# Five transposed parameter vectors leave VectorE for ScalarE, and attention's score products take the two key groups in turn

## The chip, the cores and the metric

The kernel runs on one core of a Trainium2 chip. The metric is the device time of one execution in microseconds (us); shorter is better. A core has TensorE (matmuls; PE in the profile, with PEld for its weight loads), VectorE (DVE), ScalarE (ACT), GpSimd (POOL) and SyncE (SP), which here only issues DMAs. Each engine works through its own list of instructions in order, and engines wait for each other by semaphores. Matmul results land in PSUM, in banks of 512 floats per partition.

## The reference, cut to what matters

Two layers of a decoder trunk are computed on 512 tokens of width 1024. Layer 0 has a mixer (windowed attention beside a gated short convolution), a gated MLP with a width-3 convolution, and an embedding gate. Layer 1 has the same with gated linear attention as its mixer. The attention of layer 0 is where the change acts:

```python
qb = q.reshape(b, nb, ATTN_BLOCK, ATTN_KV_HEADS, ATTN_GROUP, HEAD_DIM)   # 4 blocks of 128 queries, 2 key groups, 4 heads each, 64 wide
scores = jnp.einsum('bnqhgd,bnkhd->bnhgqk', qb, kband).astype(jnp.float32) * (HEAD_DIM ** -0.5)
...
scores = jnp.where(allowed[None, :, None, None], scores, -jnp.inf)
...
probs = jax.nn.softmax(jnp.concatenate([scores, sink], axis=-1), axis=-1)[..., :-1]
```

Each block of 128 queries sees its own 128 keys and the 128 before them (the first block only its own). The change also touches how small parameter vectors (norm gains, convolution taps and biases) come to stand along the partitions.

## The kernel before, in words

Activations stand transposed, features on partitions and the 512 tokens along the free axis. The large projections are done by `mm3` (lines 149 to 155) in three products on split operands, high by high (L153) and the two crosses of a high and a low part (L154, L155). The weights come by DMA as `raw` and are split by `cut`: ScalarE makes the high part `wh` (L133), VectorE the rest `wl` (L134). Such products, 512 wide, are the bulk of TensorE's work, and they go to PSUM tiles named `ps` (four banks). Everything smaller, transposes and attention, goes to tiles named `pa`, which are also four banks, handed round: a new `pa` tile must wait until the reader of the tile that held its bank before has finished.

`columns` (L182 to L195) turns parameter vectors: DMAs gather rows into `vrow`, TensorE transposes them into a `pa` tile (L192), and VectorE copies the result out of PSUM (L194). It is called six times: once at the start for `vec0` (with a queue given as `q`), once in mixer 0 for `vec1`, and twice in each `load_vectors_ffn` for `vfa` and `vfb` (in mixer 0 and again in mixer 1).

`mixer0` (from L357) writes its order out by hand at the end (L609 to L650). The convolution's projections (`conv_in`, 48 products each) are laid between the steps of attention so that TensorE has work while the softmax runs on the other engines. The steps are, for each block t of 128 queries:

- `query_turned(t)`: four transposes (L428), then ScalarE copies them to `qT` (L429).
- `scores(t)`: eight products (L492), one per head. Each has 64 rows of contraction: heads of key group 0 lie on partitions 0 to 63, those of group 1 on 64 to 127. Two heads share a `pa` tile, so the step takes four tiles in the order group 0 first pair, group 0 second pair, group 1 first pair, group 1 second pair. In the records each product is two matmuls. VectorE then adds the mask and takes the row maxima, one instruction per head (L500), and prepares the exponent's bias (L507, L508).
- Still in `scores(t)`: ScalarE takes eight exponentials (L514), and VectorE sums and inverts (L518, L519).
- `probs(t)`: the weights are normalized by VectorE (L528) and ScalarE (L532), transposed (L538) and copied to `pT` by ScalarE (L545) and, for the earlier keys, VectorE (L543).
- `mix(t)`: the product with the values (L554), split by ScalarE (L97) and VectorE (L98).

Around `scores(0)` the code says `query_turned(0, qn0)`, `load_vectors1()`, then two more steps, `query_turned(1, qn1)`, `scores(0)`, `conv_in("c", w)`. The `pa` banks of the four score tiles are therefore those that, in turn, the spread norm, `qT` of block 0, the turned `vec1` and `qT` of block 1 held. Within this hand order a scheduler moves single instructions of an engine against each other, so the built order can differ by a few places from the code's. Between the two projections the convolution's own work runs: `conv_taps` multiplies, pads and applies the taps (L588, L589 and L593 on VectorE, L591 on ScalarE), reading `vec1`.

In mixer 1, `load_vectors_ffn(1)` stands right before `read(2)` (L1104): products of scores and values (L1115) and of the state (L1117) into two `pa` tiles, whose squares ScalarE sums (L1119) ahead of the per-head norm; VectorE scales (L1124). A tile's second half may be written only after the squares of its first half were taken. Nearby, ScalarE applies the swish to the output gate (L890) and splits gated outputs (L97), VectorE multiplies (L889, L897).

Of the kernel before, what the change touches and what calls it, by code (L numbers as in the profile page):

```python
# [55 lines left out]
class Kernel:  # L56
# [125 lines left out]
    def columns(self, name, views, q=None):  # L182

        nc = self.nc
        n = sum(v.shape[0] for v in views)
        rows = self.sp.tile([P, P], F32, tag="vrow", name=self.nm("vrow"))
        at = 0
        for v in views:
            (q or nc.gpsimd).dma_start(rows[at : at + v.shape[0], :], v)
            at += v.shape[0]  # L190
        ps = self.pa()
        nc.tensor.transpose(ps[:, :n], rows[:n, :], self.ident[:n, :n])  # L192
        col = self.cp.tile([P, -(-n // 64) * 64], F32, name=name)[:, :n]
        nc.vector.tensor_copy(col, ps[:, :n])  # L194
        return col  # L195

    def load_vectors0(self):
# [159 lines left out]
    def mixer0(self):  # L357
        nc, a, tc = self.nc, self.a, self.tc
        with tc.tile_pool(name="m0", bufs=1) as mp:
# [15 lines left out]
            for m in range(ND):  # L375
                ps = self.ps()
# [103 lines left out]
            def scores(t):  # L480

                w = 2 * P if t else P
                k0 = (t - 1) * P if t else 0
                mask = self.amask if t else self.amask[:, P:]
                s = mp.tile([P, NQ, 2 * P], F32, tag="s", name=self.nm("s"), bufs=2)
                mx = self.few(8, "mx")
                for g in range(2):
                    for h2 in range(2):
                        pb = self.pa()
                        for hh in range(2):  # L490
                            hq = 2 * h2 + hh
                            nc.tensor.matmul(  # L492
                                pb[:, hh * 256 : hh * 256 + w],
                                qTs[t][64 * g : 64 * g + 64, hq, :],
                                kT[64 * g : 64 * g + 64, k0 : k0 + w],
                                start=True, stop=True,
                            )
                        for hh in range(2):
                            head = 4 * g + 2 * h2 + hh
                            nc.vector.tensor_tensor_reduce(  # L500
                                s[:, head, :w], pb[:, hh * 256 : hh * 256 + w], mask,
                                scale=1.0, scalar=-1e30, op0=ALU.add, op1=ALU.max,
                                accum_out=mx[:, head : head + 1],
                            )

                nm = self.few(8, "nm")
                nc.vector.scalar_tensor_tensor(out=nm, in0=mx, scalar=HD**-0.5, in1=sink, op0=ALU.mult, op1=ALU.max)  # L507
                nc.vector.tensor_scalar_mul(nm, nm, -1.0)  # L508
                den = self.few(8, "den")
                es = self.few(8, "es")  # L510
                nc.vector.tensor_tensor(es, sink, nm, ALU.add)
                nc.scalar.activation(es, es, AF.Exp)
                for head in range(NQ):
                    nc.scalar.activation(  # L514
                        s[:, head, :w], s[:, head, :w], AF.Exp, bias=nm[:, head : head + 1], scale=HD**-0.5,
                        accum_out=den[:, head : head + 1],
                    )
                nc.vector.tensor_tensor(den, den, es, ALU.add)  # L518
                nc.vector.reciprocal(den, den)  # L519
                ss[t], dens[t] = s, den  # L520
# [49 lines left out]
            def conv_w(nme, j2):  # L570
                c0 = starts[nme] + 256 * j2
                return self.weights(w_in[:, :, c0 : c0 + 256], ND, 256)
# [36 lines left out]
            w = conv_w("x", 0)  # L609
# [4 lines left out]
            w = conv_w("c", 0)  # L614
# [4 lines left out]
            qn2 = query(2)  # L619
            query_turned(1, qn1)  # L620
            scores(0)
            conv_in("c", w)
            w = conv_w("b", 0)
            conv_taps(0)
            qn3 = query(3)
            query_turned(2, qn2)
            probs(0)
            scores(1)
            conv_in("b", w)
            w = conv_w("x", 1)  # L630
            conv_out(0)
            query_turned(3, qn3)
            mix(0)
            probs(1)
            scores(2)
            conv_in("x", w)
            w = conv_w("c", 1)
# [4 lines left out]
            w = conv_w("b", 1)  # L642
# [639 lines left out]
```

## Time and profile before

| | |
|---|---|
| time, median of 3 runs (lowest to highest) | 1260.3 us (1259.97 to 1260.51) |
| time of the profiled execution | 1260.71 us |
| its span, first to last instruction | 1258.8 us |
| TensorE busy | 99% of the span |
| VectorE busy | 772.7 us, 61% |
| ScalarE busy | 541.1 us, 43% |
| mean granted TensorE clock | 0.999 |
| the five copies of turned vectors in mixers and later (L194) | 0.20 us (vec1), 0.24 us each (vfa, vfb, twice) |
| the 64 records of score products (L492) | 61.3 to 117.0 us of the span |

The span is what the traces divide up; some 1.9 us lie around it (1260.71 less 1258.8). A line of the timeline gives start, length in us, engine, code line, operation, the tiles written and read, their sizes, and in brackets how long the engine had been idle before and what ended that. A matmul's recorded length includes its way through the array, so matmuls that follow each other overlap in the records: a 512-wide product is recorded with 0.39 us, while one starts every 0.23 us. The pace is read from starts.

### The profile page before, as it was taken

The page shows a single profiled execution, that of the slowest core. Times are in us where ns is not written, and L with a number is a line of the kernel's source. Part 1 is how long each engine was busy: PE and PEld are TensorE (multiplying, and loading weights), DVE is VectorE, ACT ScalarE, POOL GpSimd, SP SyncE. Part 2 cuts the span into 40 slices and gives each one's busy share as a digit, 9 for nine tenths or more (in the row PEclk, how much of TensorE's full clock was granted, in tenths as well). Part 3 has the DMA queues.
Part 4 walks back from the last instruction along what each step waited for, and adds up shares of the span by engine and source line. Part 5 has one row for each costly group of instructions (what it writes and reads, how often), then busy time and mean ns, then how long its engine had stood idle before and what let it go on. Part 6 is the DMA issues. An engine that isn't in the chain of part 4 may idle for free.

```text
span 1258.8 us, 14853 instructions
## 1 busy us (share of the span) xinstructions
PE 1244.9 (99%) x5851; PEld 1038.1 (82%) x5851; DVE 772.7 (61%) x1190; ACT 541.1 (43%) x831; POOL 54.1 (4%) x150
## 2 busy tenths in 40 slices
PE   7999999999999999999999999999999999999998
PEld 7777788888888888888989988888888888888887
DVE  6776566777777633346679765557777777433343
ACT  6456344444444422234563544335444444232341
POOL 2500000000000000000100000000000000000000
PEclk9999999999999999999999999999999999999999
DMA  6221232333332233223322222333222233222331
GB/s 212 73 76 55 79 99 93 100 101 101 100 100 92 76 111 99 92 74 101 109 89 67 68 68 67 100 100 102 98 88 86 98 100 101 92 92 93 108 107 61
DMA packets 110473, 117.42 MB, mean 93 GB/s; under 512 B 2712, under 2 KB 105682, under 8 KB 110404
## 3 DMA queue, kind: packets, MB, share of 16 engines
q1 hardware_dynamic: 108512, 114.83, 28.0%
q10 hardware_dynamic: 1332, 1.23, 0.3%
q8 instruction: 46, 0.75, 0.2%
q0 software_dynamic: 560, 0.42, 0.2%
q14 instruction: 23, 0.19, 0.0%
HBM read 114.37 MB, written 2.10 MB: 93 GB/s over the span
## 4 chain that ended last, share of the span: by engine, by line
PE 92%; DVE 3%; ACT 2%; issue 1%; POOL 1%; DMA 1%; SPq 0%; DVEq 0%; POOLq 0%; ACTq 0%
PE ps L153 28%; PE ps L155 28%; PE ps L154 28%; PE pa L492 1%; PE pa L1001 1%; DMA xin<-in_x_dram 1%; PE pa L1115 1%; PE pa L154 1%; DVE wl L134 1%; PE pa L153 1%; PE pa L155 1%; PE pa L538 1%; PE pa L1092 0%; POOL rq L163 0%; PE pa L1117 0%
## 5 line engine op out<-in xcount | busy, mean ns | idle before, releaser
L133 ACT ACTIVATE wh<-raw 128x1024 fp32r<-128x1024 f32 (+4 forms) x222 | 224.7, 1015 | 384.5 <-PE ps L154 319.4
L134 DVE TENSOR_TENSOR wl<-raw,wh 128x1024 fp32r<-128x1024 f32 (+4 forms) x222 | 258.6, 1167 | 184.0 <-ACT wh L133 182.9
L153 PE MATMUL ps<-a,wh 128*128 128x512 f32 x864 | 337.4, 390 | 0.0
L154 PE MATMUL ps<-a,wh 128*128 128x512 f32 x864 | 337.0, 390 | 0.0
L155 PE MATMUL ps<-a,wl 128*128 128x512 f32 x864 | 336.8, 390 | 0.0
L153 PEld LDWEIGHTS ps<-a,wh 128*128 128x128 f32 x864 | 162.5, 188 | 34.3 <-issue 0.7
L155 PEld LDWEIGHTS ps<-a,wl 128*128 128x128 f32 x864 | 162.5, 188 | 34.0 <-issue 0.2
L154 PEld LDWEIGHTS ps<-a,wh 128*128 128x128 f32 x864 | 162.5, 188 | 33.8 <-issue 0.3
L682 DVE SCALAR_TENSOR_TENSOR zt<-z,vfa,zt 128x512 f32<-128x512 f32 x176 | 131.4, 749 | 3.6 <-ACT zt L680 0.6
L153 PE MATMUL ps<-b,wh 128*128 128x512 f32 x320 | 126.3, 396 | 0.6 <-ACT b L97 0.5
L155 PE MATMUL ps<-b,wl 128*128 128x512 f32 x320 | 125.3, 392 | 0.0
L154 PE MATMUL ps<-b,wh 128*128 128x512 f32 x320 | 124.9, 391 | 0.0
L679 DVE TENSOR_TENSOR z<-ps,R 128x512 f32<-128x512 f32 x88 | 60.4, 688 | 74.7 <-PE ps L155 74.7
L153 PE MATMUL ps<-ah,wh 128*128 128x512 f32 x224 | 87.1, 389 | 0.0
L154 PE MATMUL ps<-al,wh 128*128 128x512 f32 x224 | 87.1, 389 | 0.0
L155 PE MATMUL ps<-ah,wl 128*128 128x512 f32 x224 | 87.1, 389 | 0.0
L680 ACT ACTIVATE zt<-z,vfb 128x512 f32<-128x512 f32 x88 | 70.9, 807 | 5.0 <-DVE z L679 3.3
L153 PEld LDWEIGHTS ps<-b,wh 128*128 128x128 f32 x320 | 60.0, 188 | 14.0 <-ACT b L97 1.3
L155 PEld LDWEIGHTS ps<-b,wl 128*128 128x128 f32 x320 | 60.1, 188 | 12.5
L154 PEld LDWEIGHTS ps<-b,wh 128*128 128x128 f32 x320 | 60.1, 188 | 12.2
L704 ACT ACTIVATE zt<-zt 128x512 f32<-128x512 f32 x44 | 27.8, 631 | 74.8 <-DVE zt L682 74.8
L299 DVE TENSOR_TENSOR xT<-xT,ps 128x512 f32<-128x512 f32 x32 | 22.0, 688 | 57.4 <-PE ps L155 57.4
(290 smaller groups left out, 1506.1 us busy)
## 6 DMA issues: line engine op xcount, KB each, us to landing
raw<-in_ffn_w_up_dram SPq DMA_DIRECT2D x44, 1024.0 KB, 5.0
raw<-in_ffn_w_down_dram SPq DMA_DIRECT2D x16, 1024.0 KB, 5.1
raw<-in_hy_w_in_dram SPq DMA_DIRECT2D x8, 1024.0 KB, 5.0
raw<-in_ple_w_gate_dram SPq DMA_DIRECT2D x8, 1024.0 KB, 5.0
raw<-in_gla_w_in_dram SPq DMA_DIRECT2D x8, 1024.0 KB, 5.3
raw<-in_ffn_w_down_dram SPq DMA_DIRECT2D x8, 768.0 KB, 4.3
raw<-in_gla_w_out_dram SPq DMA_DIRECT2D x4, 1024.0 KB, 5.0
raw<-in_gla_w_in_dram SPq DMA_DIRECT2D x4, 672.0 KB, 4.0
```

The costliest lines, as they stand in the source:

```text
L133: nc.scalar.activation(hv, v, AF.Copy)
L134: nc.vector.tensor_tensor(lv, v, hv.bitcast(F32), ALU.subtract)
L153: mm(out, lh, rh, start=start, stop=False)
L154: mm(out, lh, rl, start=False, stop=False)
L155: mm(out, ll, rh, start=False, stop=stop)
L299: self.nc.vector.tensor_tensor(self.xT[m], self.xT[m], ps, ALU.add)
L492: nc.tensor.matmul(pb[:, hh * 256 : hh * 256 + w], qTs[t][64 * g : 64 * g + 64, hq, :], kT[64 * g : 64 * g + 64, k0 : k0 + w], start=True, ...
L538: nc.tensor.transpose(pb[:, hh * P : (hh + 1) * P], s[:, 4 * g + hh, c * P : (c + 1) * P], self.ident)
L679: nc.vector.tensor_tensor(z[:, 2:], ps, R, ALU.mult)
L680: nc.scalar.activation(y, z[:, 2:], AF.Identity, scale=w2[:, f : f + 1], bias=bb[:, f : f + 1])
L682: nc.vector.scalar_tensor_tensor(out=y, in0=z[:, tap : tap + S], scalar=w[:, f : f + 1], in1=y, op0=ALU.mult, op1=ALU.add)
L704: nc.scalar.activation(y, y, AF.Gelu)
```

## The change

Two edits. First, `columns` copies the turned rows with ScalarE unless a queue was given: only the call for `vec0` gives one, so the copies of `vec1`, `vfa` and `vfb` (five in all) go from VectorE's list to ScalarE's.

Second, `scores` takes two `pa` tiles at a time, one per key group, and alternates the groups product by product: group 0 first head, group 1 first head, group 0 second head, group 1 second head, and then the same for the second pair of heads. The maxima follow in the same order. The sums, tiles, masks and numbers of instructions are otherwise as before.

```diff
-        nc.vector.tensor_copy(col, ps[:, :n])
+        (nc.vector.tensor_copy if q else nc.scalar.copy)(col, ps[:, :n])
...
-                for g in range(2):
-                    for h2 in range(2):
-                        pb = self.pa()
-                        for hh in range(2):
-                            hq = 2 * h2 + hh
+                for h2 in range(2):
+
+                    pbs = [self.pa(), self.pa()]
+                    for hh in range(2):
+                        hq = 2 * h2 + hh
+                        for g in range(2):
                             nc.tensor.matmul(
-                                pb[:, hh * 256 : hh * 256 + w],
+                                pbs[g][:, hh * 256 : hh * 256 + w],
                                 qTs[t][64 * g : 64 * g + 64, hq, :],
                                 kT[64 * g : 64 * g + 64, k0 : k0 + w],
                                 start=True, stop=True,
                             )
-                        for hh in range(2):
+                    for hh in range(2):
+                        for g in range(2):
                             head = 4 * g + 2 * h2 + hh
                             nc.vector.tensor_tensor_reduce(
-                                s[:, head, :w], pb[:, hh * 256 : hh * 256 + w], mask,
+                                s[:, head, :w], pbs[g][:, hh * 256 : hh * 256 + w], mask,
```

In the built order the scheduler keeps the alternation in blocks 0, 1 and 3; in block 2 it puts both products of a tile together again, in the tile order group 0, group 1, group 0, group 1. ScalarE's copy of `vec1` comes to stand between its copies of `qT` of blocks 0 and 1. The copies of `vfa` and `vfb` in mixer 0 come between the splits (L97) of `mix(2)`. In mixer 1 ScalarE's order at `read(2)` becomes: `vfa`, the swish (L890), `vfb`, the first sum of squares (L1119), the split (L97), the other three; it was the first sum of squares, the swish, two more, the split, the last. TensorE's second product of `read(2)`'s first tile there moves three 512-wide products later.

## The prediction

> **What bounds the kernel now.** I read the page's busy times, then its chain of waits: TensorE is busy 99% of the span and carries 92% of the chain, so the end moves only by what TensorE loses or gains.
>
> ```profile
> PE 1244.9 (99%) x5851; PEld 1038.1 (82%) x5851; DVE 772.7 (61%) x1190; ACT 541.1 (43%) x831; POOL 54.1 (4%) x150
> ...
> PE 92%; DVE 3%; ACT 2%; issue 1%; POOL 1%; DMA 1%; SPq 0%; DVEq 0%; POOLq 0%; ACTq 0%
> ```
>
> So next the timeline, for gaps on TensorE. After the first 10 us only one is longer than 0.5 us, and the change is at it: block 0's score products.
>
> ```profile
> 60.66 1.05 ACT L429 COPY qT<-pa 128x512 f32<-128x512 f32 x2
> ...
> 61.28 0.71 PE L492 MATMUL pa<-kT,qT 64*128 64x128 f32 x4
> ...
> 62.45 1.94 POOL L163 TENSOR_TENSOR rq<-rs,mhalf 128x8 f32<-128x8 f32 x1 [1.20 <-DVE rs L162]
> ...
> 63.61 0.42 DVE L466 TENSOR_TENSOR qn<-m,rq 128x256 f32<-128x256 f32 x1
> 63.94 0.20 DVE L194 COPY vec<-pa 128x46 f32<-128x46 f32 x1
> ...
> 64.20 1.62 PE L492 MATMUL pa<-kT,qT 64*128 64x128 f32 x12 [2.21 <-DVE vec L194]
> ```
>
> Four of sixteen records run, then TensorE stands for 2.21 us until VectorE has copied `vec1` out of the bank that the next pair writes. The copy takes 0.20 us; it is late because it stands in VectorE's list behind L466, which waits for GpSimd.
>
> What follows is read from stretches of 3.41 us (stretch, length, then busy us of PE, PEld, DVE, ACT, POOL; granted clock; DMA share; GB/s):
>
> ```profile
> 6.73:10.14 3.41, 0.61 (x3) 0.61 (x4) 2.01 (x3) 1.36 (x3) 1.05 (x2) 1.00 0.93 266
> ```
> ```profile
> 61.34:64.75 3.41, 1.20 (x12) 1.01 (x13) 3.27 (x9) 2.15 (x3) 2.30 (x2) 1.00 0.78 255
> 64.75:68.17 3.42, 3.42 (x14) 2.71 (x11) 3.39 (x22) 0.01 (x1) 0.71 (x2) 0.50 0.21 66
> 68.17:71.58 3.41, 3.41 (x17) 2.78 (x16) 0.16 (x1) 3.29 (x17) 0.00 (x0) 1.00 0.02 5
> ...
> 143.25:146.67 3.42, 2.96 (x13) 1.08 (x13) 2.92 (x5) 2.02 (x4) 0.00 (x0) 1.00 0.84 238
> ```
>
> The stretch with the pause holds 1.20 us of TensorE work, and in the next the granted clock is 0.50. A lesser gap (2.96 us of work, 143.25) is followed by full clock. After the stretch from 6.73, with 0.61 us of work, 256-wide products are recorded with 0.41 us until 13.28 and with 0.28 us from 14.09: half speed there too, though its clock column shows 1.00.
>
> **The pause goes (−3.0).** On ScalarE the copy stands between the two `qT` copies. The first ends at 61.23. For the new copy I take 0.25 us (between 0.20, VectorE's for it, and 0.28, ScalarE's L97 of 128x128). The second `qT` copy, 0.5 us, ends near 61.95 instead of 61.71. The four score tiles wait for: first `qT` copy, nothing on another engine, `vec1` copy (61.5), second `qT` copy (61.95). The first pair keeps TensorE until then, the last products end their issue near 62.45, and the next 512-wide product starts some 0.30 later, as after block 1 (81.45 to 81.74): 62.75 where it is 65.74 now. Saved: 3.0.
>
> **The half clock goes (−1.1).** From 65.74 to 68.34 six steps of 512-wide products take 2.60 us; after block 1, at full clock, the same seven products start at 81.74, 82.08 and then 0.23 apart, 1.49 us. Saved 1.1 if no pause means no half clock. At the four transposes of block 2's queries, now at 77.45, TensorE is then 4.1 us early: 73.35.
>
> **Block 1 gives back 1.2.** There the same four banks were last read by: nothing, the third `qT` copy, and two `pT` copies of block 0. All these are ScalarE's, and they hang on block 0's softmax, which is not 4.1 us earlier: its maxima still stand behind L134 in VectorE's list (64.39), so the exponentials come earlier only by the 0.1 us of pitch that the copy leaves behind. ScalarE now:
>
> ```profile
> 71.98 1.06 ACT L133 ACTIVATE wh<-raw 128x1024 fp32r<-128x1024 f32 x1 [0.52 <-PE ps L154]
> ...
> 73.66 0.72 ACT L591 ACTIVATE cy<-pad,vec 128x512 f32<-128x512 f32 x1 [0.62 <-DVE pad L589]
> ...
> 74.29 1.27 ACT L532 ACTIVATE s<-s,den 128x128 f32<-128x128 f32 x4
> ...
> 77.42 1.06 ACT L133 ACTIVATE wh<-raw 128x1024 fp32r<-128x1024 f32 x1 [1.86 <-PE ps L154]
> ...
> 78.39 0.56 ACT L429 COPY qT<-pa 128x512 f32<-128x512 f32 x1
> ...
> 79.33 0.73 ACT L591 ACTIVATE cy<-pad,vec 128x512 f32<-128x512 f32 x1
> 79.95 0.58 ACT L545 COPY pT<-pa 128x512 f32<-128x512 f32 x1
> ```
>
> Exponentials end at 71.35; L133 without its wait ends its turn at 72.3, L591 at 72.95 (its input is ready), four L532 at 74.1, the next L133 at 75.1, the third `qT` copy at 75.55, the first `pT` copy at 76.0. Then L591 waits for VectorE: from the end of L528 near 72.5 come L134 (1.14), L593 twice (1.54), L588 (0.73) and L589 (0.69): 76.6. So L591 ends at 77.25 and the second `pT` copy at 77.85, only 2.7 us earlier than today's 80.53. The fourth bank's first product, and behind it in TensorE's list the rest of block 1 and the next 48 convolution products, wait for that. Three products of 0.43 us are left, two of which can run side by side: 0.87, and 0.30 to the next 512-wide one: 78.9 to 79.0, against 81.74. Of 4.1 remain 2.8 to 2.9; I take 2.9. The new gap on TensorE is about 1.1 us.
>
> **What the alternation itself is worth (0 in blocks 1 and 2, −0.2 in 3).** Heads of the two groups already overlap where they are neighbours: block 1's sixteen records of 0.216 us fill three rounds of 0.87 us, not four, for the second pair of group 0 runs beside the first of group 1 (counts include records reaching in):
>
> ```profile
> 78.84:79.71 0.87, 0.86 (x4) 0.78 (x5) 1.00 1.09 390
> 79.71:80.58 0.87, 0.87 (x10) 0.81 (x8) 1.00 0.58 203
> 80.58:81.45 0.87, 0.87 (x8) 0.74 (x4) 1.00 0.00 0
> ```
>
> Full pairing would need two rounds, 0.87 less a block. But the banks bind. In block 2 they wait for `pT` copies (one on ScalarE, two of L543) and the last L98 of `mix(0)`, whose times don't depend on the order: nothing gained. In block 3 the last L98 now stands ahead of the first maximum in VectorE's list, worth about half a 0.42 us maximum: 0.2.
>
> Here the row comes first, then a rule: three rounds, not four. The Trainium skill ("TensorEngine Tiling (Array Packing)", Theoretical Speedup) gives up to 2x for contractions of 64 rows, and its PSUM Bottleneck section says that emptying PSUM is not sped up; by the first alone three blocks would save 2.6 us more. That is the second rival below.
>
> **The other four copies (+0.2).** In mixer 0 `vfa` and `vfb` (0.24 each) go between ScalarE's L97, where ScalarE waits 0.36 and 0.52 us for VectorE; a later transpose waits for the `vfa` copy: 0 to 0.2, taken 0.05. In mixer 1 the first sum of squares, now at 748.57, comes behind `vfa`, the swish (0.62) and `vfb`, a microsecond later. TensorE's next products into that tile wait for it; three 512-wide ones (0.69) have been put before them, and 0.20 was waited already. Cost between −0.1 and 0.4; I take 0.15, since the moved products cover most. Without that cover it is 0.9. VectorE, 61% busy, loses five short copies; it bounds nothing there. The copies issue no DMA, and the weights' DMAs are tied to TensorE's pace.
>
> **Sum.** −3.0 −1.1 +1.2 +0 −0.2 +0.2 = −2.9. The profiled execution took 1260.71 us, its span 1258.8 and 1.9 around it; it becomes 1257.8. It lies 0.4 above the median of the runs, 1260.3, so the median becomes **1257.4**. Measurement can tell 0.2%, 2.5 us, so this is faster by little more than that: 1257.8 is the border.
>
> **Rivals.**
> *The new gap halves the clock again* (1259.1). Block 1's gap leaves some 2.2 us of work in its stretch, between 1.20 (halved) and 2.96 (not). If it halves, up to 3.41 us at half speed cost 1.7: 1257.4+1.7. The number lies nearer to the row without a drop.
> *No new gap, and full pairing* (1253.6 to 1256.2). If ScalarE's chain is shorter than I work out, 4.1 stay; with three blocks' full pairing 6.7. Against it: the waits above.
> *The half clock doesn't come from the pause and stays* (1257.9). Lying wholly over 512-wide products it costs 1.7 (half of 3.41) instead of 1.1, so TensorE reaches block 1 only 3.0 − 0.6 = 2.4 early, and no wait is left to shorten that. Against it: two stretches with long idling, half speed after both, and nowhere else. The Trainium skill ("TensorE: Matmul & The Clock Gate", Why this matters for your kernels) puts the limit at gaps of about 3 us; by it the 2.21 us pause would not lower the clock. The row differs: it is followed by 0.50.
> *Slower: with the groups in turn, weight loads no longer run beside products* (1267.6). Block 1's sixteen loads took 2.56 us of PEld, 0.16 each, hidden beside the products. If a change of group exposes them, a block takes 16 x (0.216 + 0.16) = 6.0 us instead of 2.6: 3.4 lost in each of blocks 0, 1 and 3, 10.2 in all: 1257.4+10.2. It makes the kernel slower from 2.9 lost in these blocks, and measurably from 5.4. For it: no row of before shows groups changing at every product. Against it: in the rounds above loads and products of the two groups run beside each other.
>
> **Chances.** Forecast 0.60 (1256.4 to 1258.4; 0.47 beyond the border of 0.2%, 0.13 within); new drop 0.17, within; no new gap 0.08, faster; clock stays 0.05, within; exposed loads 0.05, slower; what I don't see 0.05 (0.01, 0.02, 0.02). Faster 0.56, same 0.37, slower 0.07. The range takes in the forecast and the drop: 1256.1 to 1259.5.
>
> **What would show it.** L194 on ScalarE near 61.3; no gap at 62 to 64; clock 1.00 at 64.75 to 68.17; a new wait of a score product for ScalarE's `pT` copy, about 1.1 us near 77, at full clock; block 1's end near 78.9. I am wrong if that wait is nearer 3 us or 0, if records of the two groups don't start side by side, or if the sums of squares near 749 hold TensorE for over half a microsecond.

## The result, and the profile after

The changed kernel takes 1257.96 us (median of 10 runs, 1256.64 to 1259.26) against 1260.68 for the kernel before (10 runs): a ratio of 0.9977, 95% interval 0.9968 to 0.9985, or 1.9 to 4.0 us less. The forecast was 2.9 less.

Page of the changed kernel, the line of the busy times: TensorE is as full as before.

```profile
PE 1244.3 (99%) x5851; PEld 1036.7 (83%) x5851; DVE 772.0 (61%) x1185; ACT 541.6 (43%) x836; POOL 53.9 (4%) x150
```

Timeline of the changed kernel at block 0 (score products are L493 here, 512-wide products follow):

```profile
61.98 0.56 ACT L429 COPY qT<-pa 128x512 f32<-128x512 f32 x1
...
62.44 0.20 ACT L194 COPY vec<-pa 128x46 f32<-128x46 f32 x1
62.53 0.60 ACT L429 COPY qT<-pa 128x512 f32<-128x512 f32 x1
...
62.59 1.29 PE L493 MATMUL pa<-kT,qT 64*128 64x128 f32 x16
...
63.82 0.50 PE L155 MATMUL ps<-a,wl 128*128 128x512 f32 x1
```

All sixteen records run in one go; the pause of 2.21 us is gone. The copy, on ScalarE, takes the 0.20 us that it took on VectorE. (In the kernel before, the built order gave vec1's bank to the second score tile, so that only four records ran ahead of the pause; here it goes to the third. The section on the kernel before gives the banks in the order of the changed one.)

Stretches of 3.41 us of the changed kernel (columns as in the prediction): the clock stays at 1.00 where it was 0.50, and what idling there is has moved to 74.99 and 78.41.

```profile
61.34:64.75 3.41, 3.38 (x27) 2.65 (x28) 3.27 (x6) 3.39 (x6) 2.22 (x2) 1.00 0.35 98
64.75:68.17 3.42, 3.42 (x17) 2.82 (x16) 3.42 (x17) 0.17 (x1) 2.03 (x3) 1.00 0.66 227
...
74.99:78.41 3.42, 3.03 (x18) 1.73 (x17) 3.35 (x5) 2.94 (x7) 0.10 (x1) 1.00 0.61 203
78.41:81.82 3.41, 2.80 (x14) 2.11 (x15) 3.41 (x12) 0.56 (x2) 0.10 (x1) 1.00 0.30 104
```

Timeline of the changed kernel at block 1, the new wait:

```profile
76.72 0.58 ACT L547 COPY pT<-pa 128x512 f32<-128x512 f32 x1
...
77.05 0.69 DVE L591 TENSOR_TENSOR pad<-pad,cxs 128x512 f32<-128x512 f32 x1
...
77.78 0.72 ACT L593 ACTIVATE cy<-pad,vec 128x512 f32<-128x512 f32 x1 [0.48 <-DVE pad L591]
78.40 0.56 ACT L547 COPY pT<-pa 128x512 f32<-128x512 f32 x1
...
79.02 1.13 PE L493 MATMUL pa<-kT,qT 64*128 64x256 f32 x6 [0.98 <-ACT pT L547]
```

ScalarE's second pT copy stands behind L593, L593 waits for VectorE's L591, and TensorE idles 0.98 us for the copy.

The changed span, 1256.4, is only 2.4 us shorter than 1258.8, because this execution was late before the change acts: the 161st of the split products (L153 to L155), the same product in all kernels, starts at 41.66 us here and at 40.34 in the profile of before. In the ten profiles of the table below it lies between 39.56 and 41.66. So the segments are compared from that product on. The first column gives it; the others, how much earlier or later than in before the first 512-wide product behind each block of score products starts, then the products that start at 139, 619, 628, 742 and 756 us in before (behind mixer 0, around the start of layer 1, and on both sides of `read(2)`):

| us | reference | block 0 | 1 | 2 | 3 | 139 | 619 | 628 | 742 | 756 |
|---|---|---|---|---|---|---|---|---|---|---|
| before, from the reference | 40.34 | 25.41 | 41.41 | 59.39 | 76.97 | | | | | |
| changed | 41.66 | −3.25 | −2.99 | −3.05 | −3.23 | −3.17 | −3.15 | −3.54 | −3.55 | −3.44 |
| changed, second profile | 40.59 | −3.25 | −2.98 | −3.05 | −3.22 | −3.21 | −3.18 | −3.52 | −3.51 | −3.41 |
| vec1 copy alone | 41.08 | −2.83 | −2.99 | −3.03 | −3.03 | −3.04 | −3.05 | −3.47 | −3.44 | −3.48 |
| alternation alone | 39.57 | +0.31 | −0.13 | −0.20 | −0.38 | −0.35 | −0.31 | −0.54 | −0.55 | −0.59 |
| tiles in turn | 39.86 | −3.25 | −2.99 | −3.04 | −3.02 | −2.97 | −2.96 | −3.30 | −3.29 | −3.19 |
| vec1 early on VectorE | 40.50 | −1.94 | −1.37 | −1.39 | −1.39 | −1.39 | −1.33 | −1.70 | −1.69 | −1.73 |
| pT copy first | 39.56 | −3.25 | −4.19 | −3.03 | −3.18 | −3.14 | −3.13 | −3.41 | −3.13 | −3.01 |
| taps off VectorE | 41.45 | −3.25 | −4.19 | −3.15 | −3.28 | −3.27 | −3.27 | −3.23 | −3.23 | −3.11 |
| conv_out later | 39.94 | −3.25 | −4.19 | −4.28 | −4.45 | −4.45 | −4.41 | −4.54 | −4.56 | −4.46 |

Where two profiles do the same, they agree within some 0.05 us, far finer than the times of whole runs. (The two kernels with pauses further down equal the changed one through these blocks; they give −3.25 and −3.26, −2.99 both, −3.04 and −3.06, −3.19 both.) Every row is one profile, though, and all are set against the one profile of before.

### The profile page after: what moved, and what is told of

It reads as the page before. It is cut to its first block, busy times and chain, and to the rows that moved or that the text cites. A ratio compares the mean times of both kernels' runs of the same rounds, so it can differ in the third digit from the quotient of the medians.

```text
span 1256.4 us, 14855 instructions
## 1 busy us (share of the span) xinstructions
PE 1244.3 (99%) x5851; PEld 1036.7 (83%) x5851; DVE 772.0 (61%) x1185; ACT 541.6 (43%) x836; POOL 53.9 (4%) x150
## 4 chain that ended last, share of the span: by engine, by line
PE 91%; DVE 4%; ACT 2%; issue 1%; POOL 1%; DMA 1%; SPq 0%; DVEq 0%; POOLq 0%; ACTq 0%
PE ps L153 28%; PE ps L155 28%; PE ps L154 28%; PE pa L1003 1%; DVE wl L134 1%; DMA xin<-in_x_dram 1%; PE pa L154 1%; PE pa L1117 1%; PE pa L153 1%; PE pa L155 1%; PE pa L1094 0%; PE pa L493 0%; POOL rq L163 0%; PE pa L540 0%; PE pa L1119 0%
## 5 line engine op out<-in xcount | busy, mean ns | idle before, releaser
L133 ACT ACTIVATE wh<-raw 128x1024 fp32r<-128x1024 f32 (+4 forms) x222 | 224.7, 1015 | 380.7 <-PE ps L154 313.6
L134 DVE TENSOR_TENSOR wl<-raw,wh 128x1024 fp32r<-128x1024 f32 (+4 forms) x222 | 258.5, 1166 | 184.0 <-ACT wh L133 182.9
L153 PE MATMUL ps<-a,wh 128*128 128x512 f32 x864 | 337.0, 390 | 0.0
L155 PE MATMUL ps<-a,wl 128*128 128x512 f32 x864 | 336.3, 389 | 0.0
L155 PEld LDWEIGHTS ps<-a,wl 128*128 128x128 f32 x864 | 162.2, 188 | 33.9
L153 PEld LDWEIGHTS ps<-a,wh 128*128 128x128 f32 x864 | 162.2, 188 | 33.7 <-issue 0.7
L153 PE MATMUL ps<-b,wh 128*128 128x512 f32 x320 | 126.4, 396 | 0.5 <-ACT b L97 0.5
L155 PE MATMUL ps<-b,wl 128*128 128x512 f32 x320 | 125.2, 392 | 0.0
L153 PE MATMUL ps<-ah,wh 128*128 128x512 f32 x224 | 87.1, 389 | 0.0
L155 PE MATMUL ps<-ah,wl 128*128 128x512 f32 x224 | 87.1, 389 | 0.0
L153 PEld LDWEIGHTS ps<-b,wh 128*128 128x128 f32 x320 | 60.0, 188 | 13.6 <-ACT b L97 1.3
L155 PEld LDWEIGHTS ps<-b,wl 128*128 128x128 f32 x320 | 60.1, 188 | 12.4
```

The lines of the kernel that those rows point to most:

```text
L133: nc.scalar.activation(hv, v, AF.Copy)
L134: nc.vector.tensor_tensor(lv, v, hv.bitcast(F32), ALU.subtract)
L153: mm(out, lh, rh, start=start, stop=False)
L155: mm(out, ll, rh, start=False, stop=stop)
```

## The experiments

My theory: the gain is the wait for the copy of vec1 and the half clock behind it; in block 1 a wait for ScalarE gives part back; the alternation is worth 0.2 us. The main rival: the pairing of the two key groups carries the gain.

**The copy of vec1 alone** (on the kernel before):

```diff
-        nc.vector.tensor_copy(col, ps[:, :n])
+        (nc.scalar.copy if name == "vec1" else nc.vector.tensor_copy)(col, ps[:, :n])
```

> The kernel before with one edit: the copy of the turned vec1 goes to ScalarE; the other four copies and the order of the score products stay. My theory (the gain is the wait for that copy): no pause near 62 to 64, full clock after it, and a new wait of about 1 us in block 1 for ScalarE's second pT copy; block 1 ends 0.1 to 0.2 later than in the changed kernel, since the last two products after that wait are of one group, and block 3 another 0.2 later. Time 2.3 us below before (ratio 0.998). Rival (the pairing of the groups carries part of it, 0.87 us a block): 0.1 to 1.5 us below before.

Measured: 1257.61 against 1260.36, ratio 0.9977 (0.9968 to 0.9986): the whole gain. Timeline of this run at block 1:

```profile
77.19 0.72 ACT L591 ACTIVATE cy<-pad,vec 128x512 f32<-128x512 f32 x1 [0.48 <-DVE pad L589]
77.82 0.57 ACT L545 COPY pT<-pa 128x512 f32<-128x512 f32 x1
...
78.44 1.13 PE L492 MATMUL pa<-kT,qT 64*128 64x256 f32 x4 [0.55 <-ACT pT L545]
```

The same wait, shorter by 0.43 since TensorE arrives 0.42 later (block 0: −2.83 instead of −3.25). Block 1 ends alike in both, −2.99: ScalarE sets it. The 0.1 to 0.2 that I expected there isn't; the 0.2 in block 3 is.

**The alternation alone** (the changed kernel, all copies of turned vectors on VectorE):

```diff
-        (nc.vector.tensor_copy if q else nc.scalar.copy)(col, ps[:, :n])
+        nc.vector.tensor_copy(col, ps[:, :n])
```

> The changed kernel with all copies of turned vectors back on VectorE: the alternation alone. My theory: the second product now waits for VectorE's copy of vec1, so only two records of block 0 run ahead of the pause and fourteen after it; the pause stays over 2 us and the clock falls to 0.50 in the stretch after it; 0 to 0.2 us is saved in block 3. Time within 0.3 us of before (ratio 1.000). Rival (pairing): 0.9 to 2.6 us below before.

Measured: 1260.16 against 1260.36, ratio 0.9999 (0.9990 to 1.0008). Timeline of this run:

```profile
60.51 0.49 PE L493 MATMUL pa<-kT,qT 64*128 64x128 f32 x2
...
63.17 0.20 DVE L194 COPY vec<-pa 128x46 f32<-128x46 f32 x1
63.43 1.63 PEld L493 LDWEIGHTS pa<-kT,qT 64*128 64x128 f32 x14 [2.63 <-DVE vec L194]
63.43 1.93 PE L493 MATMUL pa<-kT,qT 64*128 64x128 f32 x14 [2.43 <-DVE vec L194]
```

Stretches of this run:

```profile
60.21:63.62 3.41, 0.95 (x6) 0.48 (x6) 3.27 (x8) 2.50 (x4) 2.21 (x3) 1.00 0.67 203
63.62:67.03 3.41, 3.41 (x18) 2.90 (x17) 3.41 (x21) 0.00 (x0) 1.07 (x3) 0.50 0.36 118
```

Two records, then a pause of 2.43 us, and granted clock 0.50 from 63.6 to 67.0. The alternation alone is worth 0.35 us behind block 3 by the segments (expected 0 to 0.2, and the rival's 0.9 to 2.6 is out).

**Alternation by tile** (the changed kernel):

```diff
-                    for hh in range(2):
-                        hq = 2 * h2 + hh
-                        for g in range(2):
+                    for g in range(2):
+                        for hh in range(2):
+                            hq = 2 * h2 + hh
```

> The changed kernel with the groups alternating by tile, not by product: both products of group 0's tile, then both of group 1's. My theory (records of the two groups run side by side within about four records, and the banks bind): within 0.2 us of the changed kernel. Rival (product by product is what pairs them): 0.4 to 1.3 us slower than the changed kernel, the score products of blocks 0, 1 and 3 taking longer.

Measured: 1257.15, ratio 0.9976 (0.9966 to 0.9985) to before, no different from the changed kernel. Block 0 is as quick (−3.25): records of the two groups run beside each other with two products of one tile in a row as well. Only block 3 loses 0.2.

**vec1 loaded earlier, its copy left on VectorE** (on the kernel before):

```diff
             qn0 = query(0)
+            self.load_vectors1()
             qn1 = query(1)
...
-            self.load_vectors1()
```

> The kernel before with one edit: vec1 is loaded one step earlier in the hand-written order, ahead of the second block's query, so that its copy stays on VectorE but should stand ahead of the work that waits for GpSimd. My theory (the place of the copy in a list makes the pause, not the engine): no pause near 62, no half clock, and 2.3 to 3.0 us below before, as with the copy on ScalarE. Rival (VectorE's list has no early place, or the engine itself matters): the pause stays over 1 us and the time within 1.5 us of before.

Measured: 1258.82 against 1260.70, ratio 0.9987 (0.9978 to 0.9995): 1.9 less, between theory and rival. Timeline of this run:

```profile
60.76 1.04 ACT L133 ACTIVATE wh<-raw 128x1024 fp32r<-128x1024 f32 x1
...
61.71 1.05 ACT L429 COPY qT<-pa 128x512 f32<-128x512 f32 x2
...
62.33 1.71 PE L492 MATMUL pa<-kT,qT 64*128 64x128 f32 x16 [0.85 <-ACT qT L429]
```

The wait for vec1 and the half clock are gone with the copy still on VectorE, so the engine isn't the point. But the scheduler now puts ScalarE's L133 ahead of the first qT copy: a wait of 0.85 us in its place.

**What block 1 gives back: the second pT copy ahead of L593** (the changed kernel):

```diff
-            conv_taps(0)
-            qn3 = query(3)
             query_turned(2, qn2)
             probs(0)
+            conv_taps(0)
+            qn3 = query(3)
             scores(1)
```

> The changed kernel with the convolution's taps called after the softmax weights of block 0 in the hand-written order: ScalarE then copies block 0's second pT bank right behind the first, ahead of the second L593, which waits for VectorE. My theory (what is left of the gain in block 1 is lost to that wait): the wait of 0.98 us of block 1's score products is gone or under 0.2, and the kernel is a further 0.8 to 1.0 us faster than the changed one, 3.5 to 3.7 below before. Rival (TensorE is held there by something else, or the taps now come late): within 0.2 us of the changed kernel, or slower.

Measured: 1258.15 against 1260.36, ratio 0.9982 (0.9973 to 0.9991): no faster. The first half of the theory holds: the wait for `pT` is gone (0.34 us for a `qT` copy are left) and block 1 ends at −4.19 instead of −2.99. But block 2 ends at −3.03, as ever. Timeline of this run at block 2:

```profile
90.67 0.63 ACT L97 ACTIVATE b<-cy 128x512 fp32r<-128x512 f32 x1 [0.31 <-DVE cy L605]
91.21 0.26 ACT L97 ACTIVATE b<-pa 128x128 fp32r<-128x128 f32 x1
91.37 1.06 ACT L547 COPY pT<-pa 128x512 f32<-128x512 f32 x2
...
92.00 0.66 PE L540 MATMUL pa<-cf,s 128*128 128x128 f32 x4 [0.70 <-ACT pT L547]
```

A wait of 0.70 us for another pT copy, one block on. My next theory was that VectorE, busy without a gap up to block 1's last maximum, is what comes late.

**The second group's taps off VectorE** (the changed kernel; the taps of the second channel group are also called after `scores(1)`):

```diff
                     for tap in (1, 0):
+                        if j == 1:
+                            hw = self.hconv[tap][:, j : j + 1].to_broadcast([P, S])
+                            nc.gpsimd.tensor_tensor(xs, pad[:, tap : tap + S], hw, ALU.mult)
+                            nc.gpsimd.tensor_tensor(y, y, xs, ALU.add)
+                            continue
...
-            conv_taps(0)
+            conv_taps(0, (0,))
...
             scores(1)
+            conv_taps(0, (1,))
```

> The changed kernel with two edits: ScalarE copies block 0's second pT bank right behind the first (the second taps are called after the score products of block 1), and the two tap products of that second channel group are done by GpSimd as a product and a sum each instead of VectorE. My theory (what took back the gain in the run with the pT copy first is VectorE, busy without a gap up to the last maximum of block 1, so that block 2's transposes wait for block 1's softmax): with 1.5 us of taps off VectorE the exponentials of block 1 start 1 to 1.5 us earlier, the gain of block 1 (about 1.1 us) is still there behind block 2, and the kernel is 0.8 to 1.2 us below the changed one. Rival (block 2 is held by something else, or GpSimd slows VectorE): behind block 2 no more than 0.3 us better than the changed kernel.

Measured: 1257.88 against 1260.70, ratio 0.9978 (0.9969 to 0.9987): as the changed kernel. Block 2 ends at −3.15: that theory fell. Timeline of this run:

```profile
91.72 0.69 DVE L610 TENSOR_TENSOR cy<-cy,cxs 128x512 f32<-128x512 f32 x1
...
92.44 0.63 ACT L97 ACTIVATE b<-cy 128x512 fp32r<-128x512 f32 x1 [0.82 <-DVE cy L610]
92.98 0.26 ACT L97 ACTIVATE b<-pa 128x128 fp32r<-128x128 f32 x1
93.14 1.06 ACT L547 COPY pT<-pa 128x512 f32<-128x512 f32 x2
...
93.77 0.66 PE L540 MATMUL pa<-cf,s 128*128 128x128 f32 x4 [0.74 <-ACT pT L547]
```

The softmax isn't late. The copy is, because it stands behind an L97 of `conv_out` that waits 0.82 us for VectorE: in block 2 the same pattern as in block 1.

**conv_out behind the pT copies of block 1** (the changed kernel, with the taps called as in the run before but left on VectorE):

```diff
-            conv_out(0)
             query_turned(3, qn3)
             mix(0)
             probs(1)
+            conv_out(0)
             scores(2)
```

> The changed kernel with two moves in the hand-written order: the second channel group's taps are called after the score products of block 1 (so that ScalarE copies block 0's second pT bank ahead of the second L593), and the convolution's gated output of the first half (conv_out) after the softmax weights of block 1, so that its two L97 and L98 of 512 columns stand behind block 1's pT copies and mix(0)'s splits. My theory now (in the run with taps off VectorE the gain of block 1 was lost because ScalarE's pT copy for block 2 stood behind such an L97, which waited 0.82 us for VectorE): behind block 1 and block 2 the kernel is 0.8 to 1.1 us ahead of the changed one, and so at the end: 3.9 to 4.3 us below before by the segments, 0.7 to 1.1 below the changed kernel. Rival (block 2 is held by VectorE itself, through the maxima or its own pT copies): behind block 2 within 0.3 us of the changed kernel.

Measured: 1256.46 against 1260.26, ratio 0.9971 (0.9959 to 0.9982). Block 1 −4.19, block 2 −4.28, block 3 −4.45, still −4.46 at 756: it keeps the 1.2 us that the changed kernel loses in block 1, as the theory says, a little more than the 0.8 to 1.1 expected (1.0 at 756). Beside it on the same chip the changed kernel took 1257.67; its fastest execution, 1257.22, is level with the slowest here, 1257.23. Timeline of this run:

```profile
90.44 0.59 ACT L547 COPY pT<-pa 128x512 f32<-128x512 f32 x1 [0.30 <-PE pa L540]
91.32 0.59 ACT L547 COPY pT<-pa 128x512 f32<-128x512 f32 x1 [0.29 <-PE pa L540]
...
91.96 3.16 PE L493 MATMUL pa<-kT,qT 64*128 64x256 f32 x16
```

Now the copies wait for TensorE, not TensorE for them. This is the fastest version tried.

**The changed kernel once more:**

> The changed kernel once more, beside the run with the later conv_out on the same chip. Theory: its segments from the first 512-wide products on repeat within 0.1 us (block 1's new wait 0.9 to 1.0 us, full clock after it), and what differs between executions lies ahead of them, in the first 20 us, where the clock is halved for a stretch whose end moves from run to run. Rival (the difference between executions lies in the new wait or in a clock that falls behind it in some): the wait or the clock after it differs by over 0.3 us.

Measured: 1257.67 against 1260.26, ratio 0.9979 (0.9970 to 0.9987). The wait in block 1 is 0.98 us again, the clock behind it full, and the segments repeat within 0.04. The reference product starts 1.07 us earlier than in the first profile: what differs lies ahead of it.

**Pauses put in on purpose** (the changed kernel; in `advance`, at five seams between stages, GpSimd copies the first 256 tokens of the last 128 features onto themselves):

```diff
         x = self.xT[m]
+        if m == ND - 1 and self.tags[0] in "a0b0":
+            self.site = getattr(self, "site", -1) + 1
+            for _ in range((4, 5, 5, 6, 7)[self.site] if self.site < 5 else 0):
+                nc.gpsimd.tensor_copy(x[:, :256], x[:, :256])
```

> The changed kernel with pauses put in on purpose: at five seams between stages the last 128 features pass through GpSimd copies onto themselves (4, 5, 5, 6 and 7 copies of 128x256), and everything behind waits for them. I expect TensorE gaps of some 0.8, 1.7, 1.7, 2.6 and 3.5 us (at 0.9 us a copy, less what is covered). My theory (a pause of over about 2 us inside one stretch of 3.41 us halves the clock for the next stretch, one of 1 us does not): 0.50 behind the gaps of 2.6 and 3.5, full clock behind 0.8, and the time longer by the gaps and 1.1 to 1.7 us for each drop. Rival (only gaps of about 3 us or more count, or the drop of before had another cause): no drop behind a gap of 2 to 3 us.

> As the run with rising pauses, with 7, 6, 6, 5 and 4 copies at the five seams, so that each seam gets another gap: some 3.5, 2.6, 2.6, 1.7 and 0.8 us. The theory and the rival say the same of each gap by its length, wherever it stands: 0.50 behind 2.6 and 3.5, none behind 0.8; the rival none below 3.

Measured: 1272.56 and 1278.03 (2 runs each; before 1260.70). A copy took some 0.40 us, not 0.9 (one 1.79), so the gaps came out otherwise: 1.34, 1.10, 2.37, 0.89 and 1.83 us in the first, and the clock fell behind the first, third and fourth. Neither theory nor rival sorts them by the length of a gap: 0.89 halves, 1.10 and 1.83 don't. Every stretch of half clock lasts 3.41 us or twice that, so the traces were cut into stretches of 3.41 us at those edges. Two of the seams in the first kernel:

```profile
190.78:194.19 3.41, 2.06 (x14) 1.85 (x14) 1.49 (x3) 0.46 (x1) 0.69 (x1) 1.00 0.00 0
194.19:197.60 3.41, 3.41 (x10) 2.64 (x9) 2.50 (x4) 1.15 (x2) 0.35 (x1) 0.50 0.01 2
...
552.59:556.00 3.41, 2.31 (x12) 1.62 (x10) 1.35 (x2) 1.24 (x2) 0.89 (x3) 1.00 0.63 222
556.00:559.42 3.42, 3.42 (x20) 2.95 (x20) 1.16 (x4) 1.16 (x2) 1.01 (x1) 1.00 0.02 5
```

and the TensorE work of the first (timeline):

```profile
192.16 1.05 PE L252 MATMUL pa<-ones,acc 128*128 128x1 f32 x8 [1.34 <-DVE acc L244]
193.08 0.48 PE L154 MATMUL ps<-a,wh 128*128 128x512 f32 x1
```

The page's busy times, 2.06 and 2.31, hardly differ. But 1.05 us of the first are eight products of one column each, and the second holds 512-wide products almost alone. So I count columns, at a pace estimated from these traces: 512-wide products start 0.227 us apart and 256-wide ones 0.120, so 256 columns take the difference, 0.107, and 512 take 0.213; a score product of 256 columns follows the last after 0.216, so 128 of its columns take some 0.107; one column takes next to nothing; products side by side count once. By this count every stretch of the twelve profiles sorts:

| columns pass for, of 3.41 us | stretches | next stretch |
|---|---|---|
| 0.82 (before, 61.34), 0.42 (alternation alone) | the pauses at vec1 | 0.50 |
| 0.96, 0.54, 1.12; 1.01, 0.35, 0.31, 0.62 | seams of the two kernels with pauses | 0.50 |
| 0.30, 1.07, 1.08, 1.21 | last products of four executions | 0.50 |
| 1.28, 1.38, 1.76 | last products of three other executions | 1.00 |
| 1.83, 1.86, 1.70; 1.76, 1.94 | seams of the same two kernels | 1.00 |
| 2.08, 1.79; 1.77, 1.92 | block 1's new wait, changed kernel twice and these two | 1.00 |
| 1.95 and more | all others of before, up to its last products | 1.00 |

The border lies between 1.21 and 1.28 us, a good third of a stretch. The two stretches on its sides are the ends of the run with the taps moved (first) and of the second kernel with pauses, and hold the same 256-wide products:

```profile
1251.40:1254.81 3.41, 1.54 (x13) 1.33 (x12) 0.84 (x2) 0.47 (x1) 0.00 (x0) 1.00 0.06 20
1254.81:1256.60 1.79, 0.00 (x0) 0.00 (x0) 0.00 (x0) 0.00 (x0) 0.00 (x0) 0.50 0.20 69
...
1271.45:1274.86 3.41, 1.62 (x14) 1.42 (x12) 0.85 (x2) 0.47 (x1) 0.00 (x0) 1.00 0.08 27
1274.86:1276.70 1.84, 0.00 (x0) 0.00 (x0) 0.00 (x0) 0.00 (x0) 0.00 (x0) 1.00 0.20 71
```

The length of the gap is not what counts, and recorded busy time isn't either: 1.62 us busy keep full clock here, while 2.62 at a seam of the same kernel, 1.01 by columns, lose it. Behind the third seam the half clock lasted two stretches in both kernels; the first of these passes columns worth 1.05 and 1.10 us at full clock, again under the border; those that full clock follows pass 1.55 or more.

The Trainium skill ("TensorE: Matmul & The Clock Gate", Why this matters for your kernels) tells to avoid gaps of over some 3 us; here a pause of 2.21 us did it, and a gap of 0.89 with one-column products and few 512-wide ones around it.

That the drop belonged to the pause holds for the timed runs too. The mean granted clock of an execution is recorded with three decimals: of the 70 executions of before that these experiments shared, none shows 1.000 (45 show 0.999, 25 show 0.998); of the changed kernel's 21, 15 do.

## Why the prediction was right, step by step

One reading in it was wrong, without harm to the sum: that the copy of `vec1` was late because L466 waited for GpSimd. The GpSimd instruction shown there runs until 64.39, past L466's start at 63.61; what L466 needs is the one before it, which ended at 61.25 (timeline of before, then the stretch from L134's start to the copy's end):

```profile
59.31 1.94 POOL L163 TENSOR_TENSOR rq<-rs,mhalf 128x8 f32<-128x8 f32 x1 [0.51 <-DVE rs L162]
```
```profile
59.68:64.14 4.46, 2.25 (x14) 1.41 (x12) 4.32 (x10) 3.81 (x6) 3.27 (x2) 1.00 0.45 141
```

VectorE is busy for 4.32 of these 4.46 us: the copy stood behind a list of work, not behind a wait.

- **The pause (−3.0).** −3.25 by the segments. The excess is in block 0: its sixteen records start within 1.02 us (62.60 to 63.62), and within 1.44 (62.01 to 63.45) with the copy alone. I had let the pairing gain nothing there; the copy alone gave −2.83, a little less than my 3.0. By the Trainium skill ("TensorEngine Tiling (Array Packing)", Theoretical Speedup) it would be up to twofold; sixteen records of some 0.107 us, 1.71, in 1.13 is 1.5-fold. Nothing of it reaches the end: block 1 absorbs it.
- **The half clock (−1.1).** Block 2's query transposes start at 74.38 − 41.66 = 32.72 us from the reference, 37.11 in before: 4.39 earlier, where I had 4.1; less the −3.25, 1.14 for the clock.
- **Block 1 gives back (+1.2).** Right in kind and place: −2.99 is left where I had −2.9; the wait is 0.98 us where I had 1.1, for the very copy that I named. What was given back is 4.39 − 2.99 = 1.40, not 1.2: ScalarE sets the end, so the 0.3 us by which TensorE came earlier than I had worked out were lost here too. That the gap leaves the clock alone was a chance of 0.17 against, and my ground (nearer to the row without a drop) was a guess between two rows; by columns it was 1.77 to 2.08 us of work, above the border found since.
- **Alternation (0, 0, −0.2).** −0.06 in block 2, −0.18 in block 3, and the run by tiles loses just these 0.2.
- **The other four copies (+0.05 and +0.15).** From block 3 to 139 us +0.06 and +0.01; around `read(2)`, from 742 to 756, +0.11 and +0.10. With the copy of vec1 alone it is −0.01 and −0.04.
- **Not foreseen.** Between 619 and 628 the changed kernel gains a further 0.39 and 0.34, but so do the copy alone (0.42) and the alternation alone (0.23), which have little in common; with the taps moved there is nothing of it (−3.27 to −3.23). ScalarE waits there for a DMA (`wgu`; 1.75 us in before, 1.30 in the second profile of the changed kernel). What makes the difference wasn't tried; one profile of before can't tell.

By segments the sum is −3.4, or −3.1 without the step that was not foreseen, beside my −2.9; by the medians −2.7 and −2.6, with an interval of 1.9 to 4.0 that covers both. The 2.1 us by which the reference product moves between executions are enough to blur the difference. Part of the 0.7 may lie in the one profile of before: seven of the nine rows set against it claim more than their medians, 0.47 in the mean of all nine. That is not shown, and how the 0.7 come about stays open. The rivals: pairing as the main gain, exposed weight loads, a clock drop at the new gap and a half clock without cause are each excluded by a row above.

## What to carry to other kernels

Before valuing a wait that goes, follow the banks and lists one stage on: the next late copy on the same engine takes its place, which here left 2.99 of 4.4 us, and once that one goes, another of the same kind a block later. It pays to place PSUM copies that TensorE waits for ahead of work that keeps their engine busy (VectorE's at `vec1`) or that itself waits for a third engine (ScalarE's in blocks 1 and 2); the move of a copy to another engine was only one way to do so. And where a kernel is bound by one engine all through, compare segments from a common instruction on, not whole times.

## What the runs showed of the hardware

- The clock went by columns passed in fixed stretches of 3.41 us (table above; the border between 1.21 and 1.28 us), not by the gap: one-column products, recorded as busy with 1.05 us for eight, don't keep it up.
- The start of each profiled execution runs at half speed for a while: 256-wide products are recorded with 0.41 us up to 12.05, 12.15, 13.28 and 15.38 us in four of the profiles, and with 0.28 soon after, while the clock column shows 1.00. The reference product starts at 39.56, 39.57, 40.34 and 41.66 in the same four, in the same order. Over all twelve profiles the first record of 0.28 lies between 12.52 and 16.66, and later ones by and large have the later reference product. That is the scatter of some 2 us between executions of one kernel, as far as the profiles tell.
- With GpSimd at work on 128x512 products and sums, two small VectorE instructions that read two tensors took longer in the run with the taps moved; L510 between them, which reads one, took its 0.17. Timeline of that run, where L509 takes 0.17 us and L513 0.17 in the changed kernel:

```profile
81.45 0.62 DVE L509 SCALAR_TENSOR_TENSOR nm<-mx,sink 128x8 f32<-128x8 f32 x1
...
82.13 1.29 POOL L598 TENSOR_TENSOR cy<-cy,cxs 128x512 f32<-128x512 f32 x1
...
82.31 1.13 DVE L513 TENSOR_TENSOR es<-sink,nm 128x8 f32<-128x8 f32 x1
```
